# A hybrid decoder layer on one core: RWKV's group norm by chunk, RWKV's projections first, DeltaNet's z columns later, and another rule for the choice of the next step

## The chip, the cores and the metric

The kernel runs on one core of a Trainium2 chip. The metric is the device time of one execution in microseconds (us); the kernel before takes 663.19 us (median of 3 runs, 661.61 to 666.75).

## The reference

One decoder layer on 256 tokens of width 1024, in float32: an RMS norm, one wide projection `w_in` whose columns feed four token mixers and their gates, a projection of each mixer's output, a gated sum, an output projection, and a SwiGLU feed-forward network. Cut to what the change touches:

```python
proj = rmsnorm(x, norm1_w) @ w_in          # columns: A qkv | B qkv, z, beta, a | C (RWKV) | D (Mamba) | 4 x 1024 gates
y_a = moba_attention(...)                  # A
o_b = gated_deltanet(q, k, v, beta, g)     # B: chunks of 64 tokens
y_b = rmsnorm(o_b, gdn_norm_w) * silu(b_z) # z is used only here
wkv = rwkv7_wkv(r_h, decay, k_h, v_h, kk, a_in)           # C: a recurrence over the tokens
mu, var = mean(wkv, -1), mean((wkv - mu) ** 2, -1)        # group norm: over the 64 values of a head
y_c = (wkv - mu) * rsqrt(var + 64e-5) * ln_w + ln_b
y_c = (y_c + sum(r_h * k_h * r_k, -1) * v_h) * g_out
y_d = ...                                                  # D: Mamba-2, chunks of 128 tokens
x = x + sum_n(sigmoid(gate_n) * (y_n @ w_branch[n])) @ w_out
h2 = rmsnorm(x, norm2_w); g, u = split(h2 @ ffn_w_in)
return x + (silu(g) * u) @ ffn_w_down
```

## The kernel before

**Wide products.** Every weight matrix comes in pieces of 128x1024 floats, one DMA each on SP's queue into a tile `wraw` (4 buffers). ScalarE rounds it to `whi` (3 buffers), VectorE computes the rest `wlo = wraw - whi` (3 buffers), and TensorE multiplies both with the normed input `HT`, itself held as such a pair: per output block 16 products with `whi` and 8 with `wlo`. The results lie in PSUM tiles `pj` (or `pjt`, tokens in the rows; `pbr` for a mixer's output projection), of which there are 4. So each piece costs VectorE one `wlo` subtraction, and a product on `wlo` waits for it.

**Mixers.** Beside the wide products run chains of small steps. RWKV's (`rwkv_mix`, L996) prepares its operands, turns them into token order (`ptk`), builds 64x64 blocks (`pab`, evicted by VectorE into `U` and `A3`), inverts them (`inverse`, L728: `U` goes out to DRAM as `Du` and comes back as `UL`, VectorE solves 16x16 triangles in 28 pairs of small steps on `TL` and `TLt`, these go out as `Dz` and come back as `TN`, and 32x32 products `pq`, `pt`, `pn` finish), then walks four chunks: `pA`, `pB`, `pH`, `pY`, with VectorE's `P2` and `Hn` between them. Behind the last chunk stands the group norm (L1119 on): reductions `gmean` and `gvar`, GpSimd's power `grsd`, and products on `Y` (an alias of the tile `kka`) and `Vst` (an alias of `kc`), each in two halves of 128x512. DeltaNet (`gdn_mix`, L1210) inverts and walks in the same way; its z columns are evicted to `zs` and used at its end. Attention (A) has heads `psx`, `ptp`, `po`; Mamba (D) has convolutions on VectorE (`cvt`, `bc`) and small products (`pyd`, `pty`, `ptB`); its decay masks (`decays`: `gm`, `DL`, `lm`) are made by GpSimd.

**The order.** The program is written out by a planner when it is built, and each engine runs its instructions in the order written (L181 is the one line at which every instruction is emitted, so all rows of the profile name it; tiles tell them apart). `ORD` (L23) sets the order of the wide products: `w` RWKV's small columns, `r`, `R` its two groups, `a`, `A` attention, `d`, `D` DeltaNet, `m`, `M` Mamba, `b0` to `b3` gates and output projections. `run` (L1757) keeps a model of each engine's time and takes, again and again, either the next part of the wide stream or a step of the first chain that is due. A wide part goes first if `T.behind` (TensorE has had few columns) or `T.short` says so; otherwise a due chain goes first:

```python
if b <= clock.t + EPB and (T.behind(clock.t) or T.short(clock.t)):
    cond = next(stream, 0)
```

`T.short` and `account` (L199) hold TensorE's instructions to lots of `LOT` = 128 pairs, a lot no sooner than `LOT_T` = 4.5 us after the last. `Pool.lease` and `room` tell whether a buffer may be taken, by a count per tag. `prefetch` (L392) issues DMAs, roundings and subtractions ahead, VectorE's up to `SL` = 0.25 us behind the present.

Of the kernel before, what the change touches and what calls it, by code (L numbers as in the profile page):

```python
# [21 lines left out]
T2, PIN, M2, RW, GATE, LO, HI, RAW, PJ, PA, PX, SL, EPC, EPB, HM, PG, PGS, DW, WA, WB, DEF = 4, 3, 6, 3, 2, 3, 3, 4, 4, 2, 2, 25, 30, 0, 60, 1, 0, 70, 38, 16, 0  # L22
ORD = "w_a_r_A_R_m_b0_M_d_D_b3_b2_b1"  # L23
LOT, LOT_T, SHORT = 128, 4.5, 70
# [56 lines left out]
def _order():  # L81
# [11 lines left out]
    d = [w(9 + g, 7 + g, 11 + g, 13 + g) for g in range(2)]  # L93
    m = [w(17 + g, 19 + g, 15 + g) for g in range(2)]
    b = br(1)
    e = dict(w=w(0), r=r[0], R=r[1], a=a[0], A=a[1], d=d[0], D=d[1], m=m[0], M=m[1], b0=br(0), b1=sorted(b, reverse=True, key=lambda c: c[0] == "w_in"), b2=br(2), b3=br(3))
# [21 lines left out]
class Pool:  # L118
    def __init__(self, clock, pool, bufs, psum):
        self.clock, self.pool, self.bufs, self.psum, self.tags = clock, pool, bufs, psum, {}  # L120
        self.held, self.kept = {}, set()
# [24 lines left out]
    def lease(self, shape, dtype, name, tag, bufs=None):  # L146

        self.held[tag] = self.held.get(tag, 0) + 1
        return self.tile(shape, dtype, name=name, tag=tag, bufs=bufs)

    def release(self, tag):
        self.held[tag] -= 1

    def room(self, tag, bufs=None):
        return self.held.get(tag, 0) < (bufs or self.bufs)
# [13 lines left out]
class Queue:  # L169


    def __init__(self, clock, idx, eng):
        self.clock, self.idx, self.eng, self.now, self.last, self.table = clock, idx, eng, 0.0, None, 0
        self.tick, self.cols, self.warm, self.tiling = 0, 0.0, True, (128, 128)
        self.emitted, self.lot = 0, -9.0
# [23 lines left out]
    def account(self, op, a, k, iname):  # L199
# [14 lines left out]
        if self.idx == 0:  # L214
# [5 lines left out]
            self.emitted += 1 if op == "transpose" or a[1].dtype != F32 else 2  # L220
# [95 lines left out]
def trunk(ctx: ExitStack, tc: tile.TileContext, I, out):  # L316
# [102 lines left out]
    def finish(evac, ps):  # L419

        def run(steps):
            yield from steps
            pj.release("pj")

        steps = evac(ps)
        if steps is None:
            pj.release("pj")
# [568 lines left out]
    def rwkv_mix():  # L996
# [77 lines left out]
        Y = Bb.rearrange("p q (a b) -> p (q a) b", b=64)  # L1074
        Hs = None
        V.tensor_scalar(rk2, rk2, -1.0, None, op0=OP.mult)
        for c in range(4):
# [16 lines left out]
            yield 1  # L1094
            if c < 3:
# [24 lines left out]
        hv = [slice(0, 8), slice(8, 16)]  # L1120
        for us in hv:
            V.tensor_reduce(mean[:, us], Y[:, us], op=OP.add, axis=AX.X)
            yield
        V.tensor_scalar(mean, mean, -1.0 / 64, None, op0=OP.mult)
        yield
        for us in hv:
            V.tensor_tensor(Y[:, us], Y[:, us], mean[:, us, None].to_broadcast([128, 8, 64]), op=OP.add)
            A.activation(U[:, us], Y[:, us], AF.Square)
            yield
        var = wk.tile([128, 16], F32, name="gvar", tag="gvar", bufs=1)  # L1130
        for us in hv:
            V.tensor_reduce(var[:, us], U[:, us], op=OP.add, axis=AX.X)
            yield
        V.tensor_scalar(var, var, 1.0 / 64, 64e-5, op0=OP.mult, op1=OP.add)
        yield
        rsd = wk.tile([128, 16], F32, name="grsd", tag="grsd", bufs=1)
        G.tensor_tensor(rsd, var, mh[:, :16], op=OP.pow)
        bv = Vst
        for us in hv:
            V.tensor_tensor(bv[:, us], Vst[:, us], bon[:, us, None].to_broadcast([128, 8, 64]), op=OP.mult)  # L1140
            yield
        lw = p_("lnwr").rearrange("p (q e) -> p q e", q=4)
        for us in hv:
            V.tensor_tensor(Y[:, us], Y[:, us], rsd[:, us, None].to_broadcast([128, 8, 64]), op=OP.mult)
            yield
            V.tensor_tensor(Y[:, us].rearrange("p (c q) e -> p c q e", c=2), Y[:, us].rearrange("p (c q) e -> p c q e", c=2),
# [880 lines left out]
```

## Time and profile before

| | us |
|---|---|
| timed runs: median (lowest, highest) | 663.19 (661.61, 666.75) |
| profiled execution | 669.16 |
| its span, first to last instruction | 667.4 |
| TensorE busy in it | 647.6 |
| VectorE busy | 457.4 |
| ScalarE busy | 318.3 |
| GpSimd busy | 44.5 |
| mean granted TensorE clock | 0.98 of 2.4 GHz |

A time in a view counts from the span's start. "Idle" is the time for which an engine had nothing running just before an instruction, with what ended it. Products that a view gives as float32 with narrow operands stand twice in its counts, since each is run as two records. A granted clock of 1.00 is 2.4 GHz and one of 0.50 is 1.2 GHz.

### The profile page before, as it was taken

What the parts mean: (1) busy time and instruction counts of PE and PEld (TensorE: products, weight loads), DVE (VectorE), ACT (ScalarE), POOL (GpSimd) and SP (SyncE); (2) the same over time, 40 slices, a digit from 0 to 9 for tenths busy, and PEclk for the clock granted to TensorE, in tenths of its full rate; (3) what the DMA queues carried; (4) which work ended last, traced back from release to release, by engine and by line L of the source; (5) the groups of instructions that cost most, each with busy time, mean ns of one, the idle gap of its engine ahead of it and who ended that gap; (6) DMA issues with size and microseconds to landing.
All of it is one profiled execution on the core that took longest, in us unless ns stands there. A gap on an engine that the chain in (4) does not pass through costs nothing.

```text
span 667.4 us, 15077 instructions
## 1 busy us (share of the span) xinstructions
PE 647.6 (97%) x6341; PEld 594.5 (89%) x6341; DVE 457.4 (69%) x813; ACT 318.3 (48%) x528; POOL 44.5 (7%) x48
## 2 busy tenths in 40 slices
PE   8999999899999988999999999999999999999997
PEld 7798999899898878999999989999988888888885
DVE  5575567957874379888779377767688777775443
ACT  5465465424434144566433253454565666654331
POOL 1001003003400011100210001000000000000000
PEclk9999999979997996999999999999999999999999
DMA  8444845314282123256555522665556555655651
GB/s 286 158 135 150 285 145 165 109 62 109 61 237 74 33 65 107 93 167 205 159 133 156 188 97 74 193 242 161 186 184 189 179 195 176 190 187 185 198 180 64
DMA packets 47865, 102.78 MB, mean 154 GB/s; under 512 B 19980, under 2 KB 24501, under 8 KB 47798
## 3 DMA queue, kind: packets, MB, share of 16 engines
q1 hardware_dynamic: 47562, 101.25, 47.9%
q8 instruction: 50, 0.82, 0.5%
q10 hardware_dynamic: 236, 0.58, 0.2%
q14 instruction: 17, 0.14, 0.1%
HBM read 99.17 MB, written 4.21 MB: 155 GB/s over the span
## 4 chain that ended last, share of the span: by engine, by line
PE 86%; DVE 6%; ACT 3%; issue 1%; DMA 1%; POOL 1%; DVEq 0%; ACTq 0%; POOLq 0%
PE pj L181 25%; PE pjf L181 19%; PE pd L181 9%; PE pjt L181 7%; PE pbr L181 6%; PE pjo L181 3%; PE ptk L181 2%; PE pab L181 2%; DVE wlo L181 2%; PE psx L181 1%; PE pA L181 1%; PE po L181 1%; PE pY L181 1%; PE pB L181 1%; PE pq L181 1%
## 5 line engine op out<-in xcount | busy, mean ns | idle before, releaser
L181 DVE TENSOR_TENSOR wlo<-wraw,whi 128x1024 fp32r<-128x1024 f32 x176 | 213.8, 1221 | 56.1 <-ACT whi L181 55.2
L181 ACT CAST whi<-wraw 128x1024 fp32r<-128x1024 f32 x176 | 183.1, 1049 | 140.9 <-PE pj L181 39.3
L181 PE MATMUL pj<-HT,whi 128*128 128x256 f32 x1120 | 155.1, 287 | 0.2 <-ACT HT L181 0.2
L181 PEld LDWEIGHTS pj<-HT,whi 128*128 128x128 f32 x1120 | 140.7, 190 | 4.9 <-issue 2.7
L181 PE MATMUL pjf<-HT,whi 128*128 128x512 f32 (+1 forms) x368 | 89.8, 386 | 0.0
L181 PE MATMUL pj<-HT,wlo 128*128 128x256 f32 x560 | 80.5, 284 | 0.8 <-DVE wlo L181 0.8
L181 PEld LDWEIGHTS pjf<-HT,whi 128*128 128x128 f32 x368 | 64.4, 188 | 11.2
L181 PEld LDWEIGHTS pj<-HT,wlo 128*128 128x128 f32 x560 | 71.5, 188 | 1.6 <-DVE wlo L181 1.2
L181 PE MATMUL pd<-whi,gt 128*128 128x512 f32 x176 | 54.8, 393 | 0.0
L181 PEld LDWEIGHTS pjf<-HT,wlo 128*128 128x128 f32 x352 | 48.2, 188 | 3.8
L181 PE MATMUL pjf<-HT,wlo 128*128 128x256 f32 x352 | 49.3, 281 | 0.0
L181 PEld LDWEIGHTS pd<-whi,gt 128*128 128x128 f32 x176 | 33.0, 188 | 7.4
L181 PE MATMUL pjt<-whi,HT 128*128 128x256 f32 x256 | 38.0, 302 | 0.9 <-ACT whi L181 0.9
L181 PEld LDWEIGHTS pjt<-whi,HT 128*128 128x128 f32 x256 | 35.0, 207 | 2.2 <-ACT whi L181 1.3
L181 PE MATMUL pd<-wlo,gt 128*128 128x512 f32 x88 | 34.6, 393 | 0.0
L181 DVE TENSOR_TENSOR gu<-pjf,gul 128x256 f32<-128x256 f32 x44 | 18.5, 420 | 9.0 <-ACT gul L181 9.0
L181 PE MATMUL pjt<-wlo,HT 128*128 128x256 f32 x128 | 21.0, 306 | 2.3 <-DVE wlo L181 2.3
L181 PEld LDWEIGHTS pjt<-wlo,HT 128*128 128x128 f32 x128 | 18.7, 212 | 3.0 <-DVE wlo L181 2.9
L181 DVE TENSOR_TENSOR gt<-sg,gt 128x256 fp32r<-128x256 f32 x22 | 9.4, 426 | 16.1 <-ACT gt L181 16.1
L181 PEld LDWEIGHTS pd<-wlo,gt 128*128 128x128 f32 x88 | 16.5, 188 | 3.8
L181 PE MATMUL pjo<-whi,ms 128*128 128x256 f32 x128 | 17.8, 284 | 0.0
L181 PEld LDWEIGHTS pjo<-whi,ms 128*128 128x128 f32 x128 | 16.3, 192 | 0.2 <-DVE ms L181 0.2
(397 smaller groups left out, 863.6 us busy)
## 6 DMA issues: line engine op xcount, KB each, us to landing
wraw<-in_w_in_dram SPq DMA_DIRECT2D x86, 512.0 KB, 4.2
wraw<-in_ffn_in_dram SPq DMA_DIRECT2D x44, 512.0 KB, 4.2
wraw<-in_ffn_down_dram SPq DMA_DIRECT2D x22, 512.0 KB, 4.2
wraw<-in_w_branch_dram SPq DMA_DIRECT2D x16, 512.0 KB, 5.2
wraw<-in_w_out_dram SPq DMA_DIRECT2D x8, 512.0 KB, 4.3
D<-Dv SPq DMA_DIRECT2D x1, 1536.0 KB
E<-D SPq DMA_DIRECT2D x8, 128.0 KB, 3.6
xm<-in_x_dram SPq DMA_DIRECT2D x4, 256.0 KB, 4.7
```

Of the source, the lines that this page charges most:

```text
L181: bi = fn(*a, **k)
```

## The change

1. RWKV's group norm is taken out of the place behind the fourth chunk. A chain `post` of its own is started at the second step of the first chunk and does it chunk by chunk on 128x256 pieces as soon as a chunk's `Y` is there; `g_out`'s products `pgo` come with its first chunk. RWKV's last step waits for it.
2. `ORD` puts RWKV's second group `R` directly behind its first, ahead of attention. DeltaNet's z columns (13, 14) leave `d` and `D` and come behind both; DeltaNet's mixer starts with 6 evictions in place of 8 and waits for z only at its end.
3. A wide part also goes first where VectorE's planned time is more than `VB` = 2.5 us ahead of the present.
4. The lots: the count of TensorE's instructions starts at 32 in place of 0 and each counts 1.009; `LOT_T` is 4.0 in place of 4.5. `SL` is 0.20 in place of 0.25.
5. `lease`, `release` and `room` go by the tile that would be overwritten, not by a count. Mamba's chain no longer waits for attention's end at its start, but only where it writes `yD`.

```diff
-T2, PIN, ..., PX, SL, EPC, ... = 4, 3, ..., 2, 25, 30, ...
-ORD = "w_a_r_A_R_m_b0_M_d_D_b3_b2_b1"
-LOT, LOT_T, SHORT = 128, 4.5, 70
+T2, PIN, ..., PX, SL, EPC, ... = 4, 3, ..., 2, 20, 30, ...
+ORD = "w_r_R_a_A_m_b0_M_d_D_z_b3_b2_b1"
+LOT, LOT_T, SHORT = 128, 4.0, 70
+VB = 2.5
...
-    d = [w(9 + g, 7 + g, 11 + g, 13 + g) for g in range(2)]
+    d = [w(9 + g, 7 + g, 11 + g) for g in range(2)]
...
     def room(self, tag, bufs=None):
-        return self.held.get(tag, 0) < (bufs or self.bufs)
+        line, n = self.tags.get(tag, []), bufs or self.bufs
+        return len(line) < n or line[-n] not in self.held
...
-        self.emitted, self.lot = 0, -9.0
+        self.emitted, self.lot = LOT / 4, -9.0
...
-            self.emitted += 1 if op == "transpose" or a[1].dtype != F32 else 2
+            self.emitted += 1.009 * (1 if op == "transpose" or a[1].dtype != F32 else 2)
...
+        ys = []
+        def post():
+            mean, var, rsd = [wk.tile([128, 16], F32, name=n, tag=n, bufs=1) for n in ("gmean", "gvar", "grsd")]
+            lw = p_("lnwr").rearrange("p (q e) -> p q e", q=4)
+            for c in range(4):
+                yield lambda: len(ys) > c
+                us = ys[c]
...
+                V.tensor_reduce(mean[:, us], Y[:, us], op=OP.add, axis=AX.X)
+                yield
+                V.tensor_scalar(mean[:, us], mean[:, us], -1.0 / 64, None, op0=OP.mult)
+                yield
+                V.tensor_tensor(Y[:, us], Y[:, us], bc(mean), op=OP.add)
+                y2 = wk.tile([128, 4, 64], F32, name="y2", tag="y2", bufs=1)
+                A.activation(y2, Y[:, us], AF.Square)
+                yield
+                V.tensor_reduce(var[:, us], y2, op=OP.add, axis=AX.X)
...
+                G.tensor_tensor(rsd[:, us], var[:, us], mh[:, :4], op=OP.pow)
+                V.tensor_tensor(Vst[:, us], Vst[:, us], bc(bon), op=OP.mult)
+                yield
+                V.tensor_tensor(Y[:, us], Y[:, us], bc(rsd), op=OP.mult)
+                yield
+                V.tensor_tensor(Y[:, us], Y[:, us], lw, op=OP.mult)
+                yield
+                V.tensor_tensor(Y[:, us], Y[:, us], Vst[:, us], op=OP.add)
...
+            if c == 0:
+                Chain("post", post())
...
+            ys.append(us)
             Hs = Hn
             yield 1
-
-        mean = wk.tile([128, 16], F32, name="gmean", tag="gmean", bufs=1)
...
-        yield 1
+        yield has("rwkv_post")
         yC = ytile("C")
...
+            yield has("A")
             pty = xbank("pty")[:, 0:256].rearrange("p (q t) -> p q t", q=2)
...
-            if b <= clock.t + EPB and (T.behind(clock.t) or T.short(clock.t)):
+            if b <= clock.t + EPB and (T.behind(clock.t) or T.short(clock.t) or V.now > clock.t + VB):
...
-          when(lambda: len(ready_b) == 8 and "dec" in done, then("b", gdn_mix())))
+          when(lambda: len(ready_b) == 6 and "dec" in done, then("b", gdn_mix())))
...
-          *[then(f"d{g}", when(has("A"), mam[g][1]())) for g in range(2)])
+          *[then(f"d{g}", mam[g][1]()) for g in range(2)])
```

The number of TensorE's products and of the DMAs is the same before and now; VectorE has 20 instructions more, ScalarE 2, GpSimd 3. What the planner makes of it, at three places:

**VectorE, the group norm.** Before, in the stretch where Mamba's second group is convolved (`kka` is Y, `kc` the values, `grsd` the power, `cvt` and `bc` Mamba's convolutions):

```order
L181 TENSOR_REDUCE gvar_3174<-U_1699 128x8
L181 TENSOR_SCALAR zt_1829<-zt_1829,ms_3166 128x256
L181 SCALAR_TENSOR_TENSOR cvt_3099<-pj_2738,PR_82,cvt_3099 128x255
L181 TENSOR_SCALAR gvar_3174<-gvar_3174 128x16
L181 SCALAR_TENSOR_TENSOR bc_3183<-pj_3101,PR_82,bc_3183 128x255
L181 SCALAR_TENSOR_TENSOR cvt_3099<-pj_2738,PR_82,cvt_3099 128x254
L181 TENSOR_TENSOR kc_829<-kc_829,bon_1701 128x512
L181 SCALAR_TENSOR_TENSOR yD1_3078<-pty_3201,PR_82,yD0_3077 128x128 x2
```

Now, for the second chunk, in the stretch of branch A's gates and output projections (`MT` is their sum):

```order
L185 SCALAR_TENSOR_TENSOR MT_79<-gate_2635,pbr_2730 128x512
L185 TENSOR_TENSOR wlo_2767<-wraw_2378,whi_2755 128x1024
L185 TENSOR_TENSOR kka_910<-kka_910,grsd_2633 128x256
L185 TENSOR_TENSOR kka_910<-kka_910,PR_82 128x256
L185 TENSOR_TENSOR kka_910<-kka_910,kc_563 128x256
L185 TENSOR_TENSOR wlo_2809<-wraw_2488,whi_2795 128x1024
L185 TENSOR_REDUCE gmean_2631<-kka_910 128x4
L185 TENSOR_SCALAR gmean_2631<-gmean_2631 128x4
L185 TENSOR_TENSOR kka_910<-kka_910,gmean_2631 128x256
L185 TENSOR_REDUCE gvar_2632<-y2_2830 128x4
```

The norm has moved ahead of Mamba's second group and stands between `wlo` subtractions; its first instruction stands behind the last chunk's `P2`, so it follows the recurrence on VectorE and does not run inside it.

**GpSimd.** Before, Mamba's decay masks `gm`, `DL`, `lm` come directly behind the copies and fills (`uo`, `TL`, `kkr`) of RWKV's inverse:

```order
L181 COPY uo_90<-U_1699 16x16x16 x4
L181 MEMSET TL_1969 128x256
L181 MEMSET TL_1969 128x16
L181 MEMSET kkr_1440 32x16x32 x2
L181 TENSOR_TENSOR gm_2137<-C_81,gst_244 128x512
L181 TENSOR_TENSOR DL_2138<-DL_2138,C_81 128x512
```

Now the second attention group's power `rq` comes first, and the norm's first power `grsd` stands among the masks:

```order
L185 MEMSET kkr_909 32x16x32 x2
L185 TENSOR_TENSOR rq_1754<-ss_1387,mh_72 128x16
L185 TENSOR_TENSOR gm_2713<-C_81,gst_244 128x512
L185 TENSOR_TENSOR DL_2714<-DL_2714,C_81 128x512
L185 TENSOR_TENSOR gm_2713<-C_81,gst_244 128x512
L185 TENSOR_TENSOR grsd_2633<-gvar_2632,mh_72 128x4
```

The masks have moved away from the solve and to the group norm.

**TensorE, the end of RWKV's inverse.** Before (`pq` and `pn` are its last two 32x32 stages, `pA` opens the first chunk):

```order
L181 MATMUL pq_2634<-TN_2339,U_1699 32x32 x32
L181 MATMUL pbr_2609<-yA1_264,whi_2416 128x256 x4
L181 MATMUL pbr_2609<-yA0_263,wlo_2422 128x256 x4
L181 MATMUL pn_2684<-TN_2340,TN_2341 32x32 x32
L181 MATMUL pA_2720<-kc_829,A3_1795 64x64 x8
```

Now:

```order
L185 MATMUL pq_2116<-TN_1811,U_1203 32x32 x32
L185 MATMUL pjt_1910<-wlo_1893,HT_78 128x256 x4
L185 MATMUL pj_2165<-HT_78,whi_1906 128x256 x8
L185 MATMUL pn_2176<-TN_1812,TN_1813 32x32 x32
L185 MATMUL pA_2212<-kc_563,A3_1294 64x64 x8
```

Twelve wide products stand between the two stages in place of eight.

## Rows read from the trace of the kernel before

**Rows 1.** The page: busy time of each engine in us with its share of the span, and the granted TensorE clock in 40 equal slices, in tenths.

```profile
PE 647.6 (97%) x6341; PEld 594.5 (89%) x6341; DVE 457.4 (69%) x813; ACT 318.3 (48%) x528; POOL 44.5 (7%) x48
...
PEclk9999999979997996999999999999999999999999
```

**Rows 2.** Busy time by stretch. Columns: the stretch, its length, busy us (and instructions) of PE, PEld, DVE, ACT and POOL, the granted clock, the DMA share and GB/s.

```profile
131.69:141.93 10.24, 9.53 (x54) 8.78 (x56) 6.54 (x15) 0.60 (x2) 0.00 (x0) 0.50 0.31 103
...
210.19:217.02 6.83, 6.83 (x105) 6.13 (x102) 3.62 (x8) 2.38 (x5) 0.56 (x1) 0.50 0.45 152
200.00:240.00 40.00, 38.98 (x829) 35.40 (x828) 16.16 (x31) 13.38 (x26) 1.75 (x3) 0.91 0.17 54
240.00:262.00 22.00, 16.98 (x108) 15.72 (x107) 21.26 (x45) 10.17 (x19) 3.46 (x2) 0.77 0.25 79
251.15:261.39 10.24, 8.29 (x38) 7.49 (x37) 9.98 (x18) 4.57 (x8) 1.13 (x1) 0.50 0.25 75
172.25:186.03 13.78, 13.78 (x92) 11.38 (x91) 12.79 (x32) 6.43 (x10) 7.65 (x7) 1.00 0.15 44
350.76:358.85 8.09, 7.94 (x67) 7.73 (x66) 7.09 (x32) 3.54 (x4) 0.00 (x0) 1.00 0.34 120
```

**Rows 3.** The timeline of TensorE from 118 to 146 us: start, length, what, and in brackets the idle time before it with what ended it.

```profile
127.42 1.11 PE L181 MATMUL ptp<-ident,s 128*128 128x128 f32 x6
...
129.75 0.88 PE L181 MATMUL po<-MT,pT 128*128 128x64 f32 x6 [0.75 <-ACT pT L181]
130.56 0.92 PE L181 MATMUL psx<-MT 64*128 64x256 f32 x4
132.40 1.22 PE L181 MATMUL pjt<-wlo,HT 128*128 128x256 f32 x4 [0.92 <-DVE wlo L181]
```

**Rows 4.** The same from 205 to 213 us.

```profile
209.44 0.24 PE L181 MATMUL pn<-TN 32*32 32x32 f32 x2 [0.61 <-ACT TN L181]
210.04 1.83 PE L181 MATMUL pn<-TN 32*32 32x32 f32 x62 [0.36 <-ACT TN L181]
```

**Rows 5.** The same from 240 to 265 us.

```profile
248.88 0.44 PE L181 MATMUL pty<-ident,zt 128*128 128x128 f32 x2 [2.38 <-DVE zt L181]
250.02 2.01 PE L181 MATMUL pjt<-whi,HT 128*128 128x256 f32 x12 [0.69 <-ACT whi L181]
...
253.88 0.69 PE L181 MATMUL ptk<-ident,cvt 128*128 128x128 f32 x2 [0.57 <-DVE cvt L181]
255.94 1.22 PE L181 MATMUL pjt<-wlo,HT 128*128 128x256 f32 x4 [1.37 <-DVE wlo L181]
```

**Rows 6.** VectorE's groups by form from 239.7 to 262 us: what, count, busy us, mean ns of one, idle before.

```profile
L181 DVE TENSOR_TENSOR wlo<-wraw,whi 128x1024 fp32r<-128x1024 f32 x4 | 4.9, 1218 | 0.0
...
L181 DVE TENSOR_TENSOR kka<-kka,grsd 128x512 f32<-128x512 f32 x2 | 1.4, 686 | 0.0
...
L181 DVE TENSOR_REDUCE gvar<-U 128x8 f32<-128x512 f32 x2 | 1.3, 674 | 0.0
...
L181 DVE TENSOR_SCALAR gmean<-gmean 128x16 f32<-128x16 f32 x1 | 0.2, 166 | 0.0
```

**Rows 7.** Instructions of half the width: a group of VectorE from 200 to 239.7 us, and a row of its timeline.

```profile
L181 DVE TENSOR_TENSOR P<-pB,rk 128x256 f32<-128x256 f32 x4 | 1.7, 425 | 7.6 <-PE pB L181 7.6
...
82.79 0.41 DVE L181 TENSOR_REDUCE mx<-s 128x1 f32<-128x256 f32 x1
```

**Rows 8.** The timeline of GpSimd.

```profile
172.54 1.34 POOL L181 TENSOR_TENSOR DL<-DL,C 128x512 f32<-128x512 f32 x1 [6.77 <-ACT DL L181]
...
178.05 4.04 POOL L181 TENSOR_TENSOR lm<-C,dA 128x512 f32<-128x512 f32 x4
...
233.32 0.55 POOL L181 TENSOR_TENSOR ms<-ms,mh 128x1 f32<-128x1 f32 x1 [16.24 <-DVE ms L181]
...
249.38 2.90 POOL L181 TENSOR_TENSOR grsd<-gvar,mh 128x16 f32<-128x16 f32 x1 [1.70 <-DVE gvar L181]
```

**Rows 9.** The timeline of VectorE: the last eviction ahead of RWKV's inverse, the first steps of its solve, and the same step of DeltaNet's solve.

```profile
159.24 0.55 DVE L181 TENSOR_TENSOR A<-pab,C 128x384 f32<-128x384 f32 x1
...
172.25 0.17 DVE L181 TENSOR_SCALAR TL<-UL 128x15 f32<-128x15 f32 x1
...
172.76 1.17 DVE L181 TENSOR_TENSOR TL<-TL,TLt 128x28 f32<-128x28 f32 x1
...
351.26 0.19 DVE L181 TENSOR_TENSOR TL<-TL,TLt 128x28 f32<-128x28 f32 x1
```

**Rows 10.** Pieces of the chain that ended last: start, us, what, records.

```profile
108.84 7.10 PE pj L181 x60
...
162.03 3.95 PE ptk L181 x128
```

**Rows 11.** The timeline at the start: the small activation that RWKV's first small product `pz` needs, and that product.

```profile
23.76 0.42 ACT L181 ACTIVATE thw<-cwa 64x256 f32<-64x256 f32 x1
...
24.23 1.98 PE L181 MATMUL pz<-WUP,thw 65*128 65x512 f32 x4
```

More of the change, by code (lines that the diff above doesn't have):

```diff
@@ L120, in __init__ @@
         self.clock, self.pool, self.bufs, self.psum, self.tags = clock, pool, bufs, psum, {}
-        self.held, self.kept = {}, set()
+        self.held, self.kept = set(), set()
     def keep(self, t):
@@ L146, in lease, with release @@
     def lease(self, shape, dtype, name, tag, bufs=None):
[L148 to L152, printed above, removed]
+        t = self.tile(shape, dtype, name=name, tag=tag, bufs=bufs)
+        self.held.add(t.name)
+        return t
+    def release(self, t):
+        self.held.discard(t.name)
     def room(self, tag, bufs=None):
-        return self.held.get(tag, 0) < (bufs or self.bufs)
+        line, n = self.tags.get(tag, []), bufs or self.bufs
+        return len(line) < n or line[-n] not in self.held
     def slot(self, tag, bufs=None):
@@ L422, in run @@
             yield from steps
-            pj.release("pj")
+            pj.release(ps)
         steps = evac(ps)
         if steps is None:
-            pj.release("pj")
+            pj.release(ps)
         else:
@@ L1094, in rwkv_mix @@
             yield 1
+            if c == 0:
+                Chain("post", post())
             if c < 3:
@@ L1115, in rwkv_mix @@
             A.copy(Y[:, us], pY)
+            ys.append(us)
             Hs = Hn
             yield 1
-        mean = wk.tile([128, 16], F32, name="gmean", tag="gmean", bufs=1)
[L1120 to L1146, printed above, removed]
-                            lw[:, None].to_broadcast([128, 2, 4, 64]), op=OP.mult)
-            yield
-            V.tensor_tensor(Y[:, us], Y[:, us], bv[:, us], op=OP.add)
-            yield
-        go = U.rearrange("p (q a) b -> p q (a b)", q=4)
-        for q in two:
-            pgo = bank("pgo").rearrange("p (q t) -> p q t", q=2)
-            for pp in range(2):
-                T.matmul(pgo[:, pp], GUP[:, (q.start + pp) * 128:(q.start + pp + 1) * 128], sgd, start=True, stop=True)
-            A.copy(go[:, q], pgo)
-        yield 1
+        yield has("rwkv_post")
         yC = ytile("C")
@@ L1202, in f @@
                 silu2(dst, ps, dst)
-            ready_b.append((g, i))
+            if i < 3:
+                ready_b.append((g, i))
+            done.add(f"gdn{g}{i}")
         return projT((9, 7, 11, 13)[i] + g, f)
@@ L1341, in gdn_mix @@
             yield 1
+        yield has("gdn03", "gdn13")
+        zs = gst_[3]
         for q in two:
```

26 lines of the change are left out of this document (20 added, 6 removed).

## The prediction

> **What bounds the kernel now.** The page first: TensorE is busy for 97% of the span, VectorE for 69%, and the row of the granted clock shows three places under full speed, all in the first 40% of the program [rows 1]. Since TensorE's products are the same before and now, only two things can change: TensorE's idle time, and the time for which its clock stands at 1.2 GHz. The stretches say what these cost. From 131.69 to 141.93 us the clock is 0.50 and TensorE busy for 9.53 us, from 251.15 to 261.39 busy for 8.29 us, and from 210.19 to 217.02 for 6.83 us [rows 2]; at full clock the same work takes half, so the falls cost 4.8, 4.1 and 3.4 us. Each fall stands right behind waits, which the timeline of TensorE names: 0.75 and 0.92 us for an attention tile and for a `wlo` [rows 3], 0.61 and 0.36 us for ScalarE's copies of `TN` [rows 4], and 2.38, 0.69, 0.57 and 1.37 us, of which three are for VectorE [rows 5]. Idle time and fall together:
>
> - around 130 us: 1.7 + 4.8 = 6.4 us;
> - around 210 us: 1.0 + 3.4 = 4.4 us;
> - from 248 us on: 5.0 + 4.1 = 9.2 us.
>
> That is 20.0 us of the profiled execution's 669.16. For the last place the reason is VectorE: it is busy for 21.26 of the 22.00 us from 240 to 262, while from 200 to 240, beside RWKV's recurrence, it has work for 16.16 of 40.00 [rows 2].
>
> **The group norm.** Before it is 10 products and 4 reductions of 128x512 at 0.69 and 0.67 us and 2 small steps at 0.17 [rows 6]: 6.9 + 2.7 + 0.3 = 9.9 us. Now it is 20 products of 128x256 at 0.43, 8 reductions at 0.41 and 8 small steps at 0.17 [rows 6, 7]: 8.6 + 3.3 + 1.4 = 13.3 us, so 3.4 us more work for VectorE. GpSimd's one power of 16 columns takes 2.90 us and one of a single column 0.55 [rows 8]; on the line between them a power of 4 columns is an estimated 1.0 us, so four are 4.1 us, on an engine that is busy for 7% of the span [rows 1]. ScalarE's two more squarings have its 52% of idle time for cover. What counts is the place. The order shows that the change does not do quite what its words say: the first step of the norm stands on VectorE behind the fourth chunk's `P2`, so nothing of it fills the idle 24 us of the recurrence. But it stands ahead of Mamba's second group, among branch A's gates and output projections. Up to the end of that group TensorE has 248 products `pj` and `pjt` and 96 `pbr` at 7.10 / 60 = 0.118 us [rows 10], 40.6 us without any small ones, and the norm's 13.3 us lie in that in place of 9.9 us in 22. The wait from 248 us on should go: gain 9.2 us, less 1.0 that I leave for single waits on `wlo`. Bounds: nothing gained (the backlog forms again) and all 9.2.
>
> At this place a rule speaks against the change. In RWKV's solve a step `TL` takes 1.17 us beside GpSimd's masks where the same step of DeltaNet's solve, with GpSimd idle, takes 0.19 [rows 9]; the Trainium skill, "SBUF — State Buffer", section "Who interferes with whom", says that a VectorE instruction with two inputs in SBUF and a GpSimd instruction that reads SBUF block each other for a whole instruction, and the trace agrees. By that rule the norm's products would now be held up as the solve was; what that gives is the first rival.
>
> **RWKV first.** With `R` ahead of attention the inverse begins earlier, and the wait at 132.40 us goes from its old place. What is late next is Mamba's first product on the `wlo` that stands on VectorE behind the whole solve. From the last `pab` to that product TensorE has 108 wide products (12.7 us), 96 `ptk` at 2 x 3.95 / 128 = 0.062 (5.9) [rows 10] and attention's `po`, `psx` and `ptp`, four, two and four at about 0.8, 0.9 and 0.4 (6.7) [rows 3]: 25 us, less about 1 us by which an eviction trails its product. VectorE needs from the end of its last eviction at 159.79 to the start of the solve at 172.25 us 12.5 us, mostly the three DMAs' way [rows 9], then the solve, then 1.2 us for the `wlo` [rows 6]. The solve with one `wlo` in it took 13.78 us beside 7.65 us of GpSimd's work and 8.09 us beside none [rows 2]: 12.6 or 6.9 by itself. Now only GpSimd's fills stand there, so I take 6.9: 20.6 of 24 us, no wait. With 12.6 it would be 26.3, 2.3 us late, and a fall like that at 131.69 would add 4.8. I keep 0.5 of the 6.4 us; bounds 0 and 7.1.
>
> At the end of the inverse twelve wide products stand between `pq` and `pn` in place of eight: 4 x 0.118 = 0.5 us more cover for waits of 1.0, so 0.5 us stays. Whether the clock falls there again no row tells; I keep half of the fall, 1.7 us, with bounds 0 and 3.4. Sum kept here: 2.2.
>
> At the start 20 wide products in place of 28 stand between RWKV's first product and `pz`, 0.9 us less, and `pz` began 0.05 us after the `thw` that it needs ended (24.18) [rows 11]: a new wait of up to 0.9 us, which I take whole. Behind it stand only wide products of TensorE's own queue.
>
> **The rest.** DeltaNet's mixer could start two evictions earlier, but in the order its first `ptk` still stands behind both z products; the moved pieces keep their DMAs, one each. I count 0, hidden by TensorE's wide products there; bounds the pause of a `wlo`, 1.2 us, either way [rows 6]. The lots, `SL`, `VB` and the rule for buffers act through the order alone, and what they do is in the places above.
>
> **The sum.** 20.0 - 1.0 - 0.5 - 2.2 - 0.9 = 15.4 us off 669.16, that is 653.8 for an execution like the profiled one. The median of the timed runs, 663.19, lies 5.97 under it, and the runs spread over 5.14, which is about one fall of the clock (3.4 to 4.8 us). So I take it that the middle run has one fall less, worth the mean of 4.1, and that the change can't take it away again: 15.4 - 4.1 = 11.3, 663.2 - 11.3 = 651.9, rounded 652.
>
> **Rivals.**
>
> *GpSimd's masks now hold up the norm.* Masks and the norm's first power are mixed in GpSimd's order. The solve lost 12.6 - 6.9 = 5.7 us to them [rows 2]. For it: the norm's products have two SBUF inputs like the solve's steps. Against: the solve was 56 steps of which one waited for the last, and the norm's have `wlo` and conversions from PSUM between them. If VectorE is late by 5.7, TensorE waits some 4 and the clock falls as often as not: 652 + 4 + 2 = 658. Chance 0.15.
>
> *The solve is in the way in its new place.* If its DMAs wait on SP's queue behind weight pieces for longer than before, all 2.3 us and the fall come: 652 + 7 = 659. Before, SP had its weights stand in the same way between `Du` and `UL`, which speaks against. Chance 0.12.
>
> *The clock falls more often: slower than before.* Its place is the narrow stretch from RWKV's `ptk` to the last `pY`, where attention's heads, the 32x32 stages and the chunks now lie with only four to eight wide products at a time between them. Before, falls came behind waits of 1.7, 1.0 and 5.0 us with narrow products around. Each costs 4.1 us on the mean and its wait about 1.2. With four falls more than I kept: 652 + 4 x 5.3 = 673. From two more on the gain is gone. Against it: from 141.93 to 210.19 the clock stayed at full speed through `ptk` and `pab`. Chance 0.11.
>
> *Everything goes, the falls of every run too:* 663 - 18 = 645. Chance 0.07.
>
> **How the numbers follow.** A measurement of this kernel can tell about 1%, 6.6 us, from no change: under 656.6 is faster, over 669.8 slower. The forecast has 0.55, nearly all of it (647 to 657) under 656.6; with the best case and a quarter of the first rival that makes 0.62 faster. The rest of the first two rivals and of the forecast is 0.27 within 1%, the third rival 0.11 slower. The range takes in the best case and the first two rivals to the end of their bounds: 644 to 668.
>
> **What would show it.** Right: TensorE's idle time by waits on VectorE is under 2 us ahead of 270 us, the clock stands at 0.50 in one place at most, VectorE is nowhere busy for 21 of 22 us before Mamba's second group, and the second solve's 7 us are also the first's. Wrong: `TL` steps over 0.9 us again, products of the norm over 0.6 us beside `lm`, a wait of over 2 us on the first `wlo` behind the solve, or more than two places at 0.50. TensorE's busy time should fall by as much as the halves of the falls that went.

## The result, and the profile after

The changed kernel takes 654.76 us (median of 4 runs, 652.76 to 657.62) against 663.73 for the kernel before (661.61 to 666.75): a ratio of 0.9866 with a 95% interval of 0.9832 to 0.9900. Timed once more beside e12 below it was 654.28 us, ratio 0.9847 (0.9806 to 0.9888). So it is faster by 9 us; 652 was forecast. The profiled execution took 652.76 us (span 650.9), 16.4 less than that of before.

The page of the changed kernel, answering to [rows 1]: TensorE's busy time is down by 11.9 us and its idle time from 667.4 - 647.6 = 19.8 to 650.9 - 635.7 = 15.2, and of the three low places in the row of the clock one is left.

```profile
PE 635.7 (98%) x6341; PEld 585.9 (90%) x6341; DVE 457.9 (70%) x833; ACT 318.1 (49%) x530; POOL 49.9 (8%) x51
...
PEclk9999999998999999999999999999999999999999
```

Busy time by stretch, answering to [rows 2]: the one fall of the clock, the two stretches of VectorE's load, and RWKV's solve in its new place (columns as in [rows 2]).

```profile
155.03:158.44 3.41, 3.41 (x46) 3.35 (x35) 1.89 (x4) 2.22 (x4) 0.00 (x0) 0.50 0.02 5
200.00:240.00 40.00, 40.00 (x343) 36.56 (x343) 32.13 (x63) 18.57 (x30) 15.20 (x14) 1.00 0.37 119
240.00:262.00 22.00, 22.00 (x187) 21.81 (x187) 19.78 (x36) 14.57 (x25) 1.46 (x1) 1.00 0.50 158
126.51:134.17 7.66, 6.37 (x56) 6.17 (x55) 6.70 (x35) 3.84 (x6) 1.05 (x1) 1.00 0.00 2
```

From 200 to 262 us TensorE has no idle time at all, where before it stood idle there for 1.0 + 5.0 = 6.0 us and two falls of the clock lay in the same stretch; VectorE's work has moved into 200 to 240 (32.13 us in place of 16.16). The solve takes 7.66 us in place of 13.78.

TensorE's timeline, the waits over 0.4 us behind the first 20 us, answering to [rows 3 to 5] and [rows 11], and the stage `pn` that waited before:

```profile
23.77 1.96 PE L185 MATMUL pz<-WUP,thw 65*128 65x512 f32 x4 [0.73 <-PE pj L185]
...
74.47 1.67 PE L185 MATMUL pjt<-whi,HT 128*128 128x256 f32 x12 [1.16 <-ACT whi L185]
...
129.41 0.55 PE L185 MATMUL pty<-ident,qkvo 128*128 128x128 f32 x3 [1.29 <-DVE qkvo L185]
...
137.77 0.63 PE L185 MATMUL ptq<-ident,MT 128*128 128x128 f32 x4 [0.74 <-DVE MT L185]
...
154.00 0.63 PE L185 MATMUL pjt<-wlo,HT 128*128 128x256 f32 x4 [3.07 <-issue]
...
162.02 1.20 PE L185 MATMUL pn<-TN 32*32 32x32 f32 x64
```

The waits of the three places are gone, 7.7 us, and their falls, 12.3. New waits have come, 7.0 us in the five rows above that show one. The largest, 3.07 us, has no releaser: "issue" says that TensorE waited for nothing that the profile shows. It stands in the middle of a group of wide products, and the clock falls behind it.

VectorE's timeline at the first chunk's norm, and GpSimd's `lm` there, answering to [rows 6 to 8]:

```profile
127.00 0.19 DVE L185 TENSOR_TENSOR TL<-TL,TLt 128x28 f32<-128x28 f32 x1
...
202.53 0.69 DVE L185 SCALAR_TENSOR_TENSOR MT<-gate,pbr 128x512 f32<-128x512 f32 x1 [2.00 <-PE pbr L185]
...
204.31 0.42 DVE L185 TENSOR_TENSOR kka<-kka,grsd 128x256 f32<-128x256 f32 x1
204.77 1.41 DVE L185 TENSOR_TENSOR kka<-kka,PR 128x256 f32<-128x256 f32 x1
206.21 1.15 DVE L185 TENSOR_TENSOR kka<-kka,kc 128x256 f32<-128x256 f32 x1
207.28 2.06 DVE L185 TENSOR_TENSOR wlo<-wraw,whi 128x1024 fp32r<-128x1024 f32 x1
```

```profile
205.86 5.38 POOL L185 TENSOR_TENSOR lm<-C,dA 128x512 f32<-128x512 f32 x4
```

Beside the masks the norm's products and a `wlo` are held up as the solve was before (1.41, 1.15 and 2.06 us for 0.42, 0.42 and 1.22); the step `TL` of [rows 9] is at 0.19.

### The profile page after: what moved, and what is told of

The parts are those of the page before. It is cut to its first block, busy times and chain, and to the rows that moved or that the text cites. A ratio compares the mean times of both kernels' runs of the same rounds, so it can differ in the third digit from the quotient of the medians.

```text
span 650.9 us, 15099 instructions
## 1 busy us (share of the span) xinstructions
PE 635.7 (98%) x6341; PEld 585.9 (90%) x6341; DVE 457.9 (70%) x833; ACT 318.1 (49%) x530; POOL 49.9 (8%) x51
## 4 chain that ended last, share of the span: by engine, by line
PE 85%; DVE 7%; DMA 2%; ACT 1%; issue 1%; POOL 0%; DVEq 0%; ACTq 0%
PE pj L185 23%; PE pjf L185 19%; PE pd L185 10%; PE pbr L185 7%; PE pjt L185 6%; PE pjo L185 4%; PE ptk L185 3%; DVE wlo L185 2%; PE pab L185 2%; DMA wraw<-in_w_in_dram 2%; PE pq L185 1%; PE psx L185 1%; PE pY L185 1%; PE pA L185 1%; PE pt L185 1%
## 5 line engine op out<-in xcount | busy, mean ns | idle before, releaser
L185 PEld LDWEIGHTS pjt<-whi,HT 128*128 128x128 f32 x256 | 33.2, 196 | 1.9 <-ACT whi L185 1.4
L185 PE MATMUL pjt<-wlo,HT 128*128 128x256 f32 x128 | 18.9, 283 | 3.1 <-issue 3.1
L185 PEld LDWEIGHTS pjt<-wlo,HT 128*128 128x128 f32 x128 | 16.4, 188 | 3.7 <-issue 3.3
```

Of the source, the lines that this page charges most:

```text
L185: bi = fn(*a, **k)
```

## Experiments

Twelve experiments were run; e8 is the kernel of e4 and e12 the changed kernel once more. "Ratio" is to the kernel before, with its 95% interval; "idle" is span less TensorE's busy time in the profiled execution.

| | edit | median us | ratio | idle us |
|---|---|---|---|---|
| before | | 663.73 | 1 | 19.8 |
| changed | | 654.76 | 0.9866 (0.9832 to 0.9900) | 15.2 |
| e1 | before + norm per chunk | 673.24 | 1.0130 (1.0098 to 1.0163) | 26.8 |
| e2 | before + RWKV first | 666.63 | 1.0031 (1.0008 to 1.0053) | 19.8 |
| e5 | before + both | 663.07 | 0.9985 (0.9956 to 1.0013) | 19.2 |
| e3 | changed, norm late as before | 665.11 | 1.0010 (0.9987 to 1.0033) | 19.8 |
| e6 | changed, norm late, own chain | 659.77 | 0.9952 (0.9924 to 0.9980) | 18.9 |
| e7 | changed, norm's chain first | 664.11 | 1.0007 (0.9977 to 1.0037) | 19.3 |
| e9 | changed, VB off | 658.68 | 0.9921 (0.9895 to 0.9947) | 18.9 |
| e10 | changed, old lots and SL | 663.91 | 1.0000 (0.9979 to 1.0022) | 19.1 |
| e11 | changed, loads held back | 665.73 | 1.0020 (1.0001 to 1.0040) | 22.4 |
| e4 | changed, bias loads left out | 653.81 | 0.9839 (0.9799 to 0.9879) | |
| e8 | e4's kernel, one execution | 651.75 | | 14.7 |
| e12 | changed, once more | 654.28 | 0.9847 (0.9806 to 0.9888) | 15.5 |

**e1, the norm alone.** The kernel before with the chain `post` of the diff above and nothing else.

> The kernel before with the group norm per chunk as its only edit; old order of the wide products, old lots, no VB rule. Theory by places: the wait on VectorE from 248 us on (5.0 us idle and a fall worth 4.1) goes, less 1.0 for single waits, so 8 us off: ratio to before 0.986 to 0.991, the waits and falls at 130 and 210 us stay. Rival (the gain of the change comes from the new order and not from the norm): VectorE is late at the same place or the fall comes elsewhere, ratio 0.996 to 1.003.

Measured: 1.013, 9 us slower. The place did what was expected: between 245 and 256 us the only wait left is 0.74 us. But more than that came back 30 us later: 9.0 us in four waits, and a fall of the clock of 13.65 us in which TensorE was busy for 6.75. TensorE's waits in e1 between 279 and 300 us, and the stretch of the fall:

```profile
281.67 2.40 PE L181 MATMUL py<-ident,kka 64*64 64x64 f32 x40 [2.27 <-DVE kka L181]
285.31 0.69 PE L181 MATMUL pty<-ident,zt 128*128 128x128 f32 x2 [1.24 <-DVE zt L181]
290.16 3.75 PE L181 MATMUL pj<-HT,whi 128*128 128x256 f32 x16 [4.15 <-DVE gvz L181]
299.06 1.22 PE L181 MATMUL pj<-HT,whi 128*128 128x256 f32 x8 [1.34 <-DVE KQ L181]
...
280.17:293.82 13.65, 6.75 (x59) 6.20 (x60) 10.14 (x26) 5.07 (x13) 0.55 (x1) 0.50 0.09 35
```

VectorE in e1, the norm's last step and the evictions behind it:

```profile
281.20 0.42 DVE L181 TENSOR_TENSOR kka<-kka,kc 128x256 f32<-128x256 f32 x1
...
288.34 0.87 DVE L181 SCALAR_TENSOR_TENSOR KQ<-pj,PR,KQ 128x255 f32<-128x255 f32 x2
...
289.93 0.48 DVE L181 SCALAR_TENSOR_TENSOR gvz<-pj,PR,gvz 128x255 f32<-128x255 f32 x1
```

In the old order the recurrence ends some 44 us later than in the changed kernel (its last `pY` starts at 233.6 us in e1 and at 189.7 there), and the norm, as the last chain in the list, is strung out between Mamba's convolutions until 281.6 us; DeltaNet's evictions of `pj` come behind it, and TensorE stands for a free `pj`. A wait of 2.77 us for a `wlo` at 362.98 with another fall of 6.83 us comes on top. Neither theory held: the wait moved, and grew.

**e2, the order alone.**

```diff
-ORD = "w_a_r_A_R_m_b0_M_d_D_b3_b2_b1"
+ORD = "w_r_R_a_A_m_b0_M_d_D_b3_b2_b1"
```

> The kernel before with RWKV's second group directly behind its first as its only edit; norm behind the last chunk, z columns within d and D, old lots. Theory by places: the 6.4 us at 130 and half of the 4.4 us at 210 go, the solve in its new place and the start cost up to 1.4 back, VectorE's backlog at Mamba's second group stays (9.2 us): 6 to 8 us off, ratio 0.988 to 0.992. Rival (only together with the other edits): the solve or another wait takes the place of the 130 us one, ratio 0.996 to 1.003.

Measured: 1.0031, as the rival had it. The backlog at Mamba's second group was expected to stay and is not there, so the order alone removes it; what takes its place is the end of attention. TensorE in e2, its largest wait, with the clock at 0.50 for 10.24 us around it, and VectorE just before it:

```profile
199.29 0.69 PE L181 MATMUL ptp<-ident,s 128*128 128x128 f32 x2 [3.22 <-ACT s L181]
```

```profile
195.83 0.68 DVE L181 TENSOR_REDUCE gmean<-kka 128x8 f32<-128x512 f32 x1
...
196.82 0.69 DVE L181 TENSOR_TENSOR kka<-kka,gmean 128x512 f32<-128x512 f32 x1
197.43 0.60 DVE L181 TENSOR_REDUCE mx<-s 128x1 f32<-128x256 f32 x2
```

The recurrence now ends together with attention's last head, and RWKV's chain, first in the list, puts its norm ahead of that head's `mx`.

**e3, the changed kernel with the norm put back** (the diff's `post` undone, all else kept).

> The changed kernel with the group norm put back behind the fourth chunk in halves of 128x512; all else as changed. Theory by places: VectorE is busy for over 21 of 22 us at Mamba's second group again, TensorE waits there 3 to 5 us and the clock falls once more: 7 to 9 us over the changed kernel, ratio to before 0.997 to 1.002. Rival (the rule for wide products with VectorE behind, and the earlier norm place in time, already cover it): no wait over 1 us there, ratio 0.985 to 0.990.

Measured: 1.001; the sum came as the theory of places had it, and the place did not: there is no wait over 1 us at Mamba's second group, as in e2. It is the place of e2. TensorE in e3, and GpSimd ahead of its wait:

```profile
197.17 0.88 PE L185 MATMUL po<-MT,pT 128*128 128x64 f32 x6 [0.57 <-ACT pT L185]
...
204.23 2.07 PE L185 MATMUL pd<-gm,C 128*128 128x512 f32 x2 [1.52 <-POOL gm L185]
```

```profile
200.27 2.90 POOL L185 TENSOR_TENSOR grsd<-gvar,mh 128x16 f32<-128x16 f32 x1 [61.99 <-DVE gvar L185]
203.14 1.04 POOL L185 TENSOR_TENSOR gm<-C,gst 128x512 f32<-128x512 f32 x1
```

The power in one piece stands on GpSimd ahead of the mask that TensorE wants next. So a second theory: the new order gives the norm its time, and what matters then is that it does not stand ahead of others' steps.

**e5, norm and order together**, and **e6, the old form of the norm as a chain of its own**, last in the list:

```diff
+        def post():
             mean = wk.tile([128, 16], F32, name="gmean", tag="gmean", bufs=1)
...
+            done.add("rwkv_post")
+            yield 0
+        Chain("post", post())
+        yield has("rwkv_post")
```

> The kernel before with two edits only: the norm per chunk as a chain of its own, and RWKV's second group ahead of attention; old lots, no VB rule, z within d and D, buffers by count. Theory (the two need each other: the order ends the recurrence some 45 us earlier, so that the norm, last in the list of chains, has time, and attention's end goes ahead of it): nearly the whole gain, ratio to before 0.984 to 0.991, no wait over 2 us between 190 and 300 us. Rival (lots, VB rule and buffers by tile are needed too): two stops or falls of the size of e2's come back, ratio 0.996 to 1.004.

> The changed kernel with the norm in the old form (halves of 128x512, behind the fourth chunk), but as a chain of its own, last in the list; that is e3 with only the list's place altered. Theory (what counts is that attention's last head and the masks go ahead of the norm, not its pieces): the waits for ScalarE's pT, yA and GpSimd's gm at 197 to 205 us (e3: 0.6, 0.6, 0.4 and 1.5) shrink to under 1 us together, ratio to before 0.984 to 0.991 as for the whole change. Rival (the pieces per chunk count): as e3, ratio 0.998 to 1.004.

Measured: e5 0.9985, level with before and 10 us better than e1 and 4 than e2 by the medians. The two do need each other, as the theory said, but together they are not enough, and the rival's ratio held: no wait between 190 and 300 us is over 1.01 us, but a fall of 6.83 us at 202.92 and a stop without a releaser of 2.28 us at 154.41 are there. e6 lies between the two theories at 0.9952, 5 us under e3: the list's place is worth about half. The wait for `pT`, those for `yA` and most of that for `gm` are gone. The other 5 us belong to the norm's form, its pieces and their earlier start, which is all that is left of the difference; of them the trace shows 1.7 us as waits for GpSimd's masks, 0.43, 0.28 and 0.97 us, the last in this row of TensorE's timeline, and 0.96 for a `wlo` at 301.67. Where the rest lies is not shown.

```profile
216.37 1.13 PE L185 MATMUL pl<-lm,C 128*128 128x512 f32 x2 [0.97 <-POOL lm L185]
```

**e7, the norm's chain first in the list.**

```diff
                 Chain("post", post())
+                Chain.all.insert(0, Chain.all.pop())
```

> The changed kernel with the norm's chain first in the list in place of last, so that its first three chunks stand on VectorE between the recurrence's P2 steps and only the fourth beside attention's last head. Theory A (the norm must not stand ahead of other chains' steps): the recurrence's and attention's steps wait for it, 2 to 5 us of waits of TensorE between 165 and 205 us and one fall more, ratio to before 0.991 to 0.999. Theory B (VectorE has idle time in the recurrence, 16 of 40 us busy, and takes it without loss): no wait over 0.6 us in the recurrence, ratio 0.982 to 0.988.

Measured: 1.0007. VectorE's idle time in the recurrence was filled, as the words of the change would have it, and by the medians that costs 9 us. The profile was taken of one of the fastest executions, 660.17 us at a mean clock of 0.994, where six of the ten are at 0.987, so it shows some 4 us less of it. TensorE in e7, and VectorE ahead of its first row:

```profile
190.83 0.33 PE L185 MATMUL pY<-P,A 64*64 64x64 f32 x4 [1.38 <-DVE P L185]
...
198.37 0.88 PE L185 MATMUL po<-MT,pT 128*128 128x64 f32 x6 [0.81 <-ACT pT L185]
```

```profile
190.03 0.42 DVE L185 TENSOR_TENSOR kc<-kc,bon 128x256 f32<-128x256 f32 x1
190.36 0.42 DVE L185 TENSOR_TENSOR P<-pB,rk 128x256 f32<-128x256 f32 x1
```

Theory A's mechanism held: the waits between 165 and 205 us come to 2.5 us (1.38, 0.81 and 0.31), of the 2 to 5 expected. Its fall stands at 200.36 us for 6.83, but the one behind the stop at 154 is gone, so this profile does not show one more; the ratio is just over A's range. The step `P2` (tile `P`), for which TensorE waits, stands behind the norm of the chunk before. The idle time was no free time: it came in pieces between a chain's links.

**e9, VB off** (`VB = 1e9`), and **e10, the old lots:**

```diff
-LOT, LOT_T, SHORT = 128, 4.0, 70
+LOT, LOT_T, SHORT = 128, 4.5, 70
...
-        self.emitted, self.lot = LOT / 4, -9.0
+        self.emitted, self.lot = 0, -9.0
...
-            self.emitted += 1.009 * (1 if op == "transpose" or a[1].dtype != F32 else 2)
+            self.emitted += 1 * (1 if op == "transpose" or a[1].dtype != F32 else 2)
```

(and `SL` 0.25 in e10).

> The changed kernel with VB = 1e9, so that the rule for wide products with VectorE behind never acts; the order is the same up to the end of RWKV's inverse and differs from there on. e5 (norm and order alone) was at 0.9985, so a third ingredient is needed. Theory V (it is this rule): with it off, attention's heads come ahead of the wide products in the recurrence as they did in e5, waits for pT and s of 1.5 to 3 us and a fall at 195 to 205 us come back, ratio to before 0.993 to 0.999. Theory L (it is the count of the lots): no wait over 0.6 us there, ratio 0.984 to 0.990.

> The changed kernel with the old numbers of the lots and of SL: the count of TensorE's instructions from 0 and by 1, LOT_T 4.5, SL 0.25. The order differs from the first us on. Theory L (the count of the lots is the third ingredient): the small waits of e5 at 48, 74 to 77 and 96 us (2.4 us together) and its stops without a cause at 154 and 378 us come back, ratio 0.993 to 0.999. Theory V (the rule on VectorE is): some of the early waits but none at attention's end, ratio 0.985 to 0.991.

Measured: 0.9921 and 1.0000. Each is needed: VB is worth 4 us, the numbers of the lots with `SL` 9 (which of these numbers does it was not tried). e9's waits stand where Mamba's masks are used (0.86 for `lm`, 1.20 for `Btk`), not at attention's end, so theory V's size was nearly right (0.993 was its bound) and its place wrong; 1.5 us of its profile are no matter of VB, since the fall behind the stop is 6.83 us long there and 3.41 in the changed kernel's. In e10 the small waits of e5 at 48, 74 and 96 us are back, and attention's end, and above all a stop without a releaser, each of the last two with a fall of 6.83 us. TensorE in e10:

```profile
153.03 0.31 PE L185 MATMUL pt<-TN 32*32 32x32 f32 x11 [1.17 <-issue]
...
196.16 0.90 PE L185 MATMUL ptp<-ident,s 128*128 128x128 f32 x3 [2.46 <-DVE kc L185]
...
360.38 0.85 PE L185 MATMUL pt<-TN 32*32 32x32 f32 x43 [2.74 <-issue]
```

The changed kernel has the second stop too, at 362.24 us, with 0.16 us.

**e4 and e8, what the stop of 3.07 us is.** Attention's second group uses the bias tiles of the first; the order on the four engines is the same.

```diff
+            if g == 1:
+                E = es[1 + h % 3]
+                SY.account("dma_start", (E, src), {}, None)
+                return E
```

> The changed kernel without the four loads of attention's second group of bias tiles E (4 x 128 KB between 142.9 and 149.5 us); the tiles of the first group are used again, and the order on TensorE, VectorE, ScalarE and GpSimd is the same word for word. It leaves those loads out. Theory: the 3.07 us in which TensorE stood at 151 to 154 us with nothing to wait for was its next piece of instructions, queued behind loads (the DMA engines were at 0.79 to 1.06 of their time); with 0.5 MB less in front at 235 to 415 GB/s the stop is 1.3 to 2.2 us shorter, 0.9 to 1.8 us, and the fall behind it may go. Rival: the stop hangs on the place in TensorE's instructions alone and stays 2.8 to 3.3 us.

> The kernel of e4 (without the second group's four loads of E, same order on the four engines), for its trace at the granted clock of the others: the profile of e4 had a clock of 0.75 throughout and shows nothing on the stop. Theory (piece of instructions queued behind loads): the stop at some 151 us is 0.9 to 1.8 us. Rival: 2.8 to 3.3 us as in the changed kernel.

Measured: e4's five timed runs beside the profiled one gave 0.9839 (0.9799 to 0.9879), no clear difference from the changed kernel, and its profile has a granted clock of 0.75 nearly throughout, so it can't be set beside the others. In e8 the stop is 1.94 us. That is under 3.07, but kernels that kept the loads and have the same order up to there show 2.08 to 2.48, so the loads of `E` are not shown to be the cause. What the trace's transfer records do show is the place of the stop in each (us; "due" is TensorE's record 1491, where the changed count makes 32 + 1.009 x 1491 = 12 lots of 128; "piece" is the next transfer of the page's instruction queue q8, which brings 0.82 MB in 50 pieces, 16 KB each):

```
            due      piece starts  ends     TensorE goes on   start - due   stop
changed     147.04   151.71        152.65   154.00            4.67          3.07
e3          148.41   152.29        153.16   154.72            3.88          2.41
e6          152.41   155.95        156.84   158.38            3.54          2.08
e7          147.41   151.41        152.30   153.78            4.00          2.48
e9          148.26   152.34        153.22   154.61            4.08          2.45
e12         152.14   156.00        156.90   158.34            3.86          2.31
e8          149.04   152.61        153.51   154.87            3.57          1.94
```

In each the stop is the piece's delay less 1.5 to 1.6 us, and TensorE goes on 1.35 to 1.56 us after the piece has landed. It stops in front of record 1617, 126 records behind the due one. In e2, e5 and e10, whose order there is another, it stops in front of record 1618, in the middle of `pt`: the place hangs on the count of instructions and not on the tile. The same link to a landing holds wherever a profile names "issue" for TensorE: in the kernel before, the changed one and all experiments but e4 there are 22 such stops, of 0.10 to 3.07 us, and behind each TensorE goes on 1.2 to 1.6 us after a piece of q8 has landed (1.28 for the 0.17 us at 198.03 in the kernel before, 1.42 for the 2.74 us of e10). Four of the five later pieces of the changed kernel between 160 and 185 us start 0.4 to 0.8 us after they are due, the fifth before it, and there is no stop at them. So the traces show the stop as a late piece of instructions; no run moved the piece and nothing else. TensorE ran dry at 150.93 us, 3.9 us after the due record, where a lot in the recurrence lasts 5.2 to 6.9 us.

Why the piece was late is open. In the changed kernel TensorE, VectorE, ScalarE and GpSimd had no work from 151 to 154 us, and the DMA engines were at 0.79 to 1.06 of their time from 150 to 152 (the second to last column is their share):

```profile
150.00:151.00 1.00, 0.93 (x8) 0.85 (x8) 0.04 (x1) 0.00 (x0) 0.00 (x0) 1.00 0.79 287
151.00:152.00 1.00, 0.00 (x0) 0.00 (x0) 0.00 (x0) 0.00 (x0) 0.00 (x0) 1.00 1.06 415
152.00:153.00 1.00, 0.00 (x0) 0.00 (x0) 0.00 (x0) 0.00 (x0) 0.00 (x0) 1.00 0.69 257
```

But in e8, without the loads of `E`, SP issued its weight pieces earlier and the engines were at 0.78 to 1.00 from 147 to 152 us all the same, so e8 did not take the load off the engines.

**e11, weight loads held back.**

```diff
-                if q >= RAW and pieces[q - RAW].stage < 3 or SY.now > clock.t + 1.0 and n > 2:
+                if q >= RAW and pieces[q - RAW].stage < 3 or n > 2 and (SY.now > clock.t + 1.0 or clock.bus > clock.t + 1.5):
```

> The changed kernel with weight loads held back while the DMA engines are planned more than 1.5 us behind: at the end of the inverse each weight load is issued later and attention's second pair of E ahead of the branch's weights; TensorE's order differs from there on. Theory Q (the stop of 3.07 us is a piece of instructions behind queued loads): the stop at 150 to 155 us is under 1 us and the piece starts within 1.5 us of its place, ratio to before 0.978 to 0.985. Rival (a late weight costs more than the stop): new waits for whi or TN of over 2 us, ratio 0.987 to 0.996.

Measured: 1.002, worse than both theories had it. The stop is gone, and the piece starts 1.39 us after record 1491, so that by the table's rule (delay less 1.5) there is none to expect. But the order at this place is another one too, so this does not prove what made the piece late. It was paid for elsewhere, though not where the rival had it: 1.80 us for `MT` at 198 and 1.49 for `lm` at 220, 1.37 for a `wlo` at 310, and 1.71 us of "issue" at 370; for `whi` it is 1.95 at most.

**e12, the changed kernel once more.**

> The changed kernel itself once more, since its first four times lie in two groups (652.8 and 652.8; 656.7 and 657.6, at a mean clock of 0.997 and 0.992) and all parts were compared with few of its runs. Theory P: the groups differ by one fall of the clock, 3.4 to 5.1 us, and its place is the new wait for pz at 24 us, behind which the clock fell for 6.83 us in e6 and e11 but not in the first profile of the changed kernel; median 653 to 657, ratio to before 0.984 to 0.990, and a profile at 0.992 shows 0.50 at 24 to 35 us. Rival: the second fall stands at the wait for whi at 74 us or behind the stop at 154 us.

Measured: median 654.28, and the profile caught an execution of 656.73 us at a mean clock of 0.992. Theory P held for this execution: besides the fall at 160 us there is one of 6.83 us at 0.50 behind the wait for `pz`. (Its other part over the first profile is the wait at 79 us, 2.08 in place of 1.16, less 0.8 at the stop.) TensorE's timeline in e12; the eight `pq` took 1.99 us in the first profile:

```profile
24.51 1.95 PE L185 MATMUL pz<-WUP,thw 65*128 65x512 f32 x4 [0.73 <-PE pj L185]
26.40 3.35 PE L185 MATMUL pq<-cwa,AUP 64*128 64x256 f32 x8
```

The stretch of the fall in e12:

```profile
26.87:33.70 6.83, 6.83 (x27) 5.73 (x26) 1.56 (x2) 1.91 (x5) 0.00 (x0) 0.50 0.24 89
```

## Why the prediction was right, step by step

**The sum.** 15.4 us off the profiled execution were forecast, 16.4 came. It is right in size in part by luck, because errors cancel. Waits and falls at the three old places went whole, 20.0 us, as said. For what comes in their place 4.6 us were kept, of which 1.7 for a fall; the five rows above are 7.0 us and the fall 3.41 / 2 = 1.7, so 8.7. Against that some 3.4 us of small waits elsewhere went ([rows 3 to 5] held only the three places), 0.5 us at the program's end and 1.3 us of busy time that no fall accounts for; none of these had a term.

**The group norm.** The forecast for its place was right: no wait from 240 to 262 us, VectorE at 19.78 of 22. One sign of being right was missed by a little: waits on VectorE ahead of 270 us, put at under 2 us, are 2.3 behind the first 30 us (1.29, 0.74 and 0.29). The step that failed is the attribution of the 9.2 us to the norm: e1 shows that the norm alone makes 9 us more, and e3 that with the new order the backlog does not form even with the norm late, but hits attention's end. The gain belongs to the pair, and e5, e9 and e10 show that it takes the lots and VB besides. The z columns, the buffers by tile and the old order within the changed kernel were not tried by themselves. Nor does a full VectorE make a backlog by itself, as the reading of the last place took it to do: in the changed kernel it is busy for 21.44 of the 22.00 us from 278 to 300, and TensorE waits for it there for 0.38 us. What counts is whose step stands behind whose.

**The rival of the masks.** The hold-up exists: five of the six instructions of VectorE from 204.8 to 211.5 us took together 3.7 us longer than the same ones elsewhere, where 5.7 was put, and GpSimd's four `lm` took 5.38 us in place of 4.04. TensorE did not wait for it: VectorE had 2.00 us of idle time just before (at 202.53), was idle again for 0.54 at 212.06, and TensorE had wide products of its own. "Products of the norm over 0.6 us beside `lm`" was named as a sign of failure and was none. By the rule of the Trainium skill, "SBUF — State Buffer", section "Who interferes with whom", a VectorE instruction with two inputs in SBUF and a GpSimd instruction that reads SBUF block each other. The trace agrees with it for the four of the five that have two such inputs; the fifth, a step of 128x4 on `gmean` with one, took 0.56 us for 0.17 all the same. The masks did cost something at another place, which the prediction had not: the first `gm`, now directly behind `rq` (133.12 to 136.08), holds up the attention product that TensorE waits for at 137.77, which takes 1.52 us where its second half takes 0.68 at 138.69.

```profile
136.04 1.04 POOL L185 TENSOR_TENSOR gm<-C,gst 128x512 f32<-128x512 f32 x1
...
136.11 1.52 DVE L185 TENSOR_TENSOR MT<-MT,rq 128x512 f32<-128x512 f32 x1 [0.80 <-POOL rq L185]
```

The 0.84 us lost here are more than the 0.74 us of that wait.

**RWKV first.** The solve without masks took 7.66 us with two of attention's instructions in it (6.9 by itself was taken), and the first `wlo` behind it was not waited for. But attention's `qkvo`, which I did not list among what is queued with the solve on VectorE, was: 1.29 us at 129.41, and 0.74 for `MT` at 137.77. I had kept 0.5, so this term was too small by 1.5. That the `wlo` was in time is a narrow thing. From the end of the last eviction (110.30) to the start of the solve (126.51) it took 16.2 us and not 12.5; so the `wlo` was ready 25.0 us behind that eviction and not 20.6, at 135.32, and TensorE came to it at 136.39, after having stood for 1.29 itself. Without that wait it would have come at about the same time as the `wlo`. The reason is the one of the rival "the solve is in the way", in a smaller size: `UL` was issued 10.4 us behind `Du`, where before it was 5.55 (161.41 and 166.96), because a weight piece ahead of it on SP's queue waited for 8.4 us.

```profile
109.91 1.72 SPq L185 DMA_DIRECT2D Du<-U  x2
...
119.86 0.36 SPq L185 DMA_DIRECT2D wraw<-in_w_in_dram  x1
120.33 1.31 SPq L185 DMA_DIRECT2D UL<-Du  x2
```

The product that `qkvo` needs had ended at 128.01, and its turn among the solve's steps came at 129.08; with the solve as early as forecast most of the 1.29 us would be saved, by an estimate from these rows. No run tried it.

**The end of the inverse.** 2.2 us were kept for waits for `TN` and half a fall. `pn` has no wait at all; the 3.07 us of "issue" and 1.7 of a fall take their place. The term was mis-sized by 2.6 us and its mechanism was missed: the dense 32x32 products took up most of 126 records in 3.9 us, and the next piece of instructions came later than that. A row of this kind stood in the trace before, with 0.17 us at 198 us, and I passed over it.

**The start.** 0.9 us were taken for `pz`, 0.73 came. The fall behind it, which e12's execution has and the first profiled one has not, was not foreseen. The median was put at 11.3 us by taking one fall of before out, and came at 9.0; a fall of 3.4 us in some executions is the likely rest, though only two executions of the changed kernel were seen in a profile.

**Not foreseen at all:** the wait of 1.16 us at 74.47 (2.08 in e12). The chain that ended last has it as one piece, a weight load that is issued right behind attention's 1.5 MB `D` and lands after 10.57 us:

```profile
62.70 10.57 DMA wraw<-in_w_in_dram
```

## What to carry to other kernels

In a program whose order is planned, a part's worth is no property of the part: here the edits make 9 us together; with the norm's place, the VB rule or the numbers of the lots undone, from 0 to 5 us of it are left, and the norm alone cost 9 us. Ask of a step that is moved not only where it finds idle time but whose step stands behind it in that engine's queue: an engine that is idle between the links of a chain is not free. The same holds for a DMA queue: a weight load that has to wait holds up the small transfer behind it. And count what one stretch asks of the instruction supply: here TensorE took 126 records, most of them 32x32 products, in 3.9 us and then ran dry.

## What the runs showed of the hardware beyond this

- A stop of TensorE that the profile puts down to "issue" goes with a late piece of its instructions: at record 1617 its length went with the delay of the piece's start in seven profiles (1.94 us at 3.57, 3.07 at 4.67), and behind all 22 such stops TensorE went on 1.2 to 1.6 us after a piece of q8 had landed. What makes the piece late is open.
- The same wait does not always bring a fall of the clock. Behind 0.73 us, with `pz` and `pq` on 65 and 64 partitions after it, the clock fell for 6.83 us in e6, e11 and e12 and not in the first profile of the changed kernel, e3, e7, e8 and e9; behind 1.29 us at 129 us it fell in none of the profiles with that wait; and behind the stop at 154 us it fell in the changed kernel, e3, e9 and e12 and not in e6, e7 and e8. So single profiles of one kernel can differ by 3.4 us for one fall of 6.83 us.
